# One chain of heads across the blocks of a hybrid encoder layer, S5 constants in parts

## The chip, the cores and the metric

The kernel runs on one core of a Trainium2 chip. The metric is the device time of one execution in microseconds (us), lower being better. Engines are named as in the profile: PE is the matmul engine (TensorE), DVE is VectorE, ACT is ScalarE, POOL is GpSimd, and SP is SyncE, which issues nearly all DMAs here. "L120" is line 120 of the kernel before, unless the text says that it speaks of the changed one; behind line 292 a line of the changed kernel has a higher number (L813 has become L820, L852 has become L859, L1126 has become L1133).

## The reference

One layer of a streaming encoder, for 2048 tokens of a prompt and 32 tokens of a second group. All groups of heads read the same normalised input, and their outputs share one output projection:

```python
hn = rmsnorm(h, W['norm_mix'][i])
proj = hn @ W['w_in'][i]
qkv_pre, z, ba, u5, cc = jnp.split(proj, [OFF_Z, OFF_BA, OFF_S5, OFF_CC], axis=-1)
ya, s_gdn, b_gconv = gdn_mixer(qkv_pre, z, ba, ...)      # gated delta rule, 4 heads x 128, short conv
yb, s_s5 = s5_mixer(u5, ...)                             # diagonal state space scan, then a GLU
yc, b_conv = conformer_conv(cc, ...)                     # GLU, depthwise conv of width 31, LayerNorm, silu
mix = jnp.concatenate([ya, yb, yc], axis=-1)
h = h + mix @ W['w_out'][i]
hf = rmsnorm(h, W['norm_ffn'][i])
h = h + (jax.nn.silu(hf @ W['ffn_w1'][i]) * (hf @ W['ffn_w3'][i])) @ W['ffn_w2'][i]
h = h + (p[i] @ W['pe_w'][i]) * jax.nn.sigmoid(h @ W['pe_gate_w'][i])
```

The model has width 1024 and a hidden width of 2816. The gated delta rule and the S5 scan carry a state over the tokens; the convolution of width 31 needs the 30 rows ahead. Everything is in float32. Outputs are the normalised result and the new states of both groups.

## The kernel before

Tokens come in four blocks (b = 0 to 3) of 512; the last one has 32 more, the second group, and its products go in two pieces of 272 columns. Features lie on the partitions. A dense product (`dense`, L104) is made of three float32r products per block of 128 features: high part of the weight by high part of the input, low by high, and high by low. A product of eight features' blocks is thus 24 matmuls into one PSUM buffer; there are three such buffers, so PE can be three products ahead of their eviction. `load_weight` (L81) brings a weight: a load on SP, the high part by ACT (L94), the low part by POOL (L96) the first time, with a store that keeps it in DRAM (L100), and by a load of that (L93) in all later blocks.

The dense work has two phases. Phase A (`PhaseA.block`, L622) makes for each block the normalised input, then the products for S5 (u5), the gates of the delta rule (`gates`, whose last part ends in ps_gc, L780), the conformer's gated input xc, twelve weights of q, k and v with a short convolution behind each (`conv`, L592: raw, three taps on gacc, a tanh and a product), and four weights of z (zz, L730 and L733). Phase F (`PhaseF.block`, L1107; F0 to F3 below) loads the mixed heads of a block as hb (L1124), splits them into fah and fal, multiplies by w_out, and then makes the hidden layer (w1 and w3 by L1165 to L1173, w2 by L1187) and the gated embedding. F0 splits its weights on POOL; F1 to F3 load the low parts that F0 kept.

The heads themselves are generators, and they run between the dense products:
- `conformer_block` (conf_b): 62 taps of the depthwise convolution on DVE (two halves of 31, L813 and the operation ahead of it, accumulating in cacc), transposes on PE (ps_ct, L824), statistics, transposes back (ps_cf, L843), and two halves of the output (L846 to L852), cxn, which SP stores to mixT, the buffer in DRAM from which phase F loads hb. There is one buffer cxn, so that the second half waits for the first one's store.
- `gdn_group` (twice for each block; gdn_b): the chunked delta rule, whose first matmul with the solved chunk is ps_q (L982), behind a triangular solve on DVE that ends in XT (L961).
- `s5_init`: the constants of S5, made once (powers of lambda, PTre and PTim, the small convolution kernel kg and ps_kg, L352).
- `s5_unit` (S5_0 for blocks 0 and 1, S5_1 for blocks 2 and 3): four quarters, each with matmuls ps_v (L459), a scan and products on DVE and POOL that end in X and XD (L498, L500), and matmuls ps_y (L517, L518); after two quarters gq (L537), which the products of the GLU read (ps_glu, L547).

Two things set the order. First, `dense` calls `step`, which counts columns of matmuls, and after each STAGE = 9216 columns (18 matmuls of 512) moves every started chain on by one stage; `yield k` takes k stages. `flush` runs the chains to their end. Second, instructions have priorities by class ("first" ahead of "heads" ahead of "later"; weights are first, dense matmuls and the chains are later), and a scheduler makes from them, from the dependences and from the memory of the pools one fixed order for every engine. Each engine then runs its instructions in this order and waits at each for what it needs. A pool on the right side (R, for each head) takes memory that an earlier pool has freed.

In the kernel before, s5_init runs in one go between block 0 and block 1 of phase A, in the class "heads". One chain of conf_0 and gdn_0 is started behind it, S5_0 is started as a second chain ahead of block 2, and the chains are flushed behind block 3. Ahead of each F block b a chain of conf and gdn of block b + 1 is started, with S5_1 at the end of that of F0, and it is flushed behind the block.

Of the kernel before, what the change touches and what calls it, by code (L numbers as in the profile page):

```python
# [206 lines left out]
def s5_init(G, A, tp, pspool):  # L207
# [78 lines left out]
    for m in (1, 2, 4):  # L286
# [4 lines left out]
        cmul(nc, tmp, Lre[:, m + 1:2 * m + 1], Lim[:, m + 1:2 * m + 1], Lre[:, 1:m + 1], Lim[:, 1:m + 1], bre, bim)  # L291


    nre = t8("nre")
# [23 lines left out]
    cmul(nc, [x[:, :, :16] for x in big], Bre, Bim, bre0, bim0, bc(kre), bc(kim))  # L318


    C.Hre = cp.tile([P, 8, 9, 16], F32, tag="Hre", name="Hre")
# [3 lines left out]
    for l in range(9):  # L325
        tmp = [x[:, :, l * 16:(l + 1) * 16] for x in big]
        cmul(nc, tmp, C.Hre[:, :, l], C.nHim[:, :, l], cre0, cim0, bc(Lre[:, l]), bc(Lim[:, l]))
    V.tensor_scalar(C.nHim, C.nHim, -1.0, None, op0=ALU.mult)
    for l in range(8):
        tmp = [x[:, :, l * 16:(l + 1) * 16] for x in big]  # L330
        cmul(nc, tmp, Pre[:, :, l], Pim[:, :, l], Bre, Bim, bc(Lre[:, l]), bc(Lim[:, l]), eng=nc.gpsimd)

    C.PT = []
    for nm, src in (("PTre", Pre), ("PTim", Pim)):
# [25 lines left out]
    for l in range(8):  # L360
        nc.sync.dma_start(C.Toep[l * 16:(l + 1) * 16, :, (7 - l) * 16:P].rearrange("p g (l c) -> p g l c", c=16), kg[:, :, 0:l + 1])


    NC = G.UB * BLK // L5
# [11 lines left out]
    while m < NC:  # L376
        s3 = [P, 8, m]
        tmp = [x.rearrange("p a b -> p (a b)")[:, :8 * m].rearrange("p (a b) -> p a b", a=8) for x in big]
        cmul(nc, tmp, fre[:, :, m:2 * m], fim[:, :, m:2 * m], fre[:, :, 0:m], fim[:, :, 0:m],
             fre[:, :, m - 1:m].to_broadcast(s3), fim[:, :, m - 1:m].to_broadcast(s3))  # L380
        m *= 2
    a = big[0][:, :, :NC]
    b = big[1][:, :, :NC]
# [31 lines left out]
def s5_unit(G, A, u, wp, pspool):  # L415
# [14 lines left out]
    for jq in range(4):  # L430
# [17 lines left out]

        yield 2

# [54 lines left out]

        yield 2

        ys = wp.tile([P, 4, NCT], F32, tag="ys", name="ys")
        ysv = ys.rearrange("p (j h) c -> p j h c", h=2)
        for j0 in (0,):  # L510
            for h in range(2):
                p_ = pspool.tile([P, 512], F32, tag="pc", name="ps_y")
                for j in range(j0, j0 + 2):
                    g = 2 * j + h
# [22 lines left out]
        V.scalar_tensor_tensor(gq[:, jh], t, 1.0, yf, op0=ALU.add, op1=ALU.mult)  # L537
        yield 2
    spc = 512 // NCT
# [23 lines left out]
class PhaseA:  # L563
# [58 lines left out]
    def block(self, b):  # L622
# [76 lines left out]
        for j in range(2):  # L699
# [13 lines left out]
            if not last:  # L713
                nc.sync.dma_start(G.xcd[b + 1][:, j, 0:30], xc[:, BLK - 30:BLK])
        with G.later():
            for g in gs:
                for _ in g:
                    pass
        for h in range(NH):
            self.conv(4 + h, 2 * h, b, hf, hl_, bc, n, last, t0)  # L720
            self.conv(h, 2 * h + 1, b, hf, hl_, bc, n, last, t0)
        for h in range(NH):
            self.conv(8 + h, 8 + h, b, hf, hl_, bc, n, last, t0)
        for h in range(NH):
            w = load_weight(G, A.w_in[12 + h], KD, "z", h)
# [129 lines left out]
def gdn_group(G, A, sp, pspool, T, tw, nt, nw, S, b, c_out):  # L855
# [105 lines left out]
    V.transpose(XT.rearrange("p w c -> p (w c)"), X.rearrange("p w c -> p (w c)"))  # L961
    yield 3

# [263 lines left out]
def trunk_kernel(ctx: ExitStack, tc: tile.TileContext, A):  # L1227
    nc = tc.nc
    G = Ctx()
# [36 lines left out]

    def flush():
        while G.chains:
            G.chains = [c for c in G.chains if advance(c)]
# [101 lines left out]
    with ExitStack() as cx:  # L1371
        pa = PhaseA(G, A, cx)
        pa.block(0)
        with R("s5i") as tp, G.heads():
            s5_init(G, A, tp, G.psM)

        with R("s5_0") as w5:
            G.start(run(conf_of(0), gdn_of(0)))
            for b in range(1, NB):
                if b == G.UB:  # L1380
                    G.start(s5_unit(G, A, 0, w5, G.psM))
                pa.block(b)
            if NB == G.UB:
                G.start(s5_unit(G, A, 0, w5, G.psM))
            G.flush()
    pf = PhaseF(G, A, ctx)
    for b in range(NB):
        nb = b + 1
        if nb < NB:

            G.start(run(conf_of(nb), gdn_of(nb), *(s5_of(u) for u in range(1, G.NU) if max(u * G.UB - 2, 0) == b)))
        pf.block(b)
        G.flush()

# [114 lines left out]
```

## Time and profile before

| what | us |
|---|---|
| timed runs, lowest / median / highest | 2912.3 / 2914.17 / 2915.87 |
| the profiled execution: its own time | 2906.6 |
| the profiled execution: its span | 2904.8 |
| PE busy, share of the span | 2775.6, 96% |
| DVE busy | 1769.2, 61% |
| ACT busy / POOL busy | 931.4 / 625.4 |
| mean granted clock of PE | 0.976 of full speed |

The span runs from the first to the last instruction; the profiled execution's own time is 1.8 longer, and the median of the timed runs is 7.6 above that. A row of the timeline gives the start, the length, the engine, the line and the operation as out<-in, the count, and in brackets how long the engine had stood idle and what released it. A row of the groups gives the busy time and the mean in ns behind the first bar. A row of the windows gives start:end, the length, and the busy time of PE, of its weight loads, of DVE, ACT and POOL, with counts, then the granted clock, the share of the DMA engines and GB/s. Phase A ends at some 706 us, with the last product of z; F0 ends at about 1300.

### The profile page before, as it was taken

How to read it: one execution, taken by the hardware profiler on the slowest of the kernel's cores; microseconds unless marked ns; L12 is line 12 of the kernel's file. 1: busy time of each engine (PE TensorE's matmuls, PEld its weight loads, DVE VectorE, ACT ScalarE, POOL GpSimd, SP SyncE). 2: the span in 40 equal slices, each digit the busy share in tenths (PEclk: the TensorE clock that was granted, in tenths of full speed). 3: DMA queues.
4: the chain of work that ended last, by engine and by line, in shares of the span. 5: the costliest groups of instructions: out<-in, count | busy, mean ns of one | idle time of the engine just before them, and what ended most of it. 6: DMA issues, size and time to landing. Idle time of an engine off the chain costs nothing.

```text
span 2904.8 us, 40874 instructions
## 1 busy us (share of the span) xinstructions
PE 2775.6 (96%) x15300; PEld 2373.5 (82%) x15300; DVE 1769.2 (61%) x3812; ACT 931.4 (32%) x1382; POOL 625.4 (22%) x482
## 2 busy tenths in 40 slices
PE   7789999899999999898999999999999999999997
PEld 5668777798878778676888887888888789999997
DVE  8989768896675856676663645954454543333343
ACT  4244433334322222233322323432222343222232
POOL 5733222133543434441010100110000010000000
PEclk9989999999999999899999999999999999999998
DMA  6577776657654546565565656765565574555553
GB/s 217 186 261 245 234 206 222 190 169 242 218 176 161 187 152 225 172 205 204 190 199 160 208 167 222 243 203 179 186 190 167 178 269 158 175 174 175 175 188 104
DMA packets 280566, 565.16 MB, mean 195 GB/s; under 512 B 68993, under 2 KB 128529, under 8 KB 280225
## 3 DMA queue, kind: packets, MB, share of 16 engines
q1 hardware_dynamic: 280368, 562.55, 60.1%
q8 instruction: 121, 1.98, 0.3%
q14 instruction: 77, 0.62, 0.1%
HBM read 457.67 MB, written 104.20 MB: 193 GB/s over the span
## 4 chain that ended last, share of the span: by engine, by line
PE 73%; DVE 14%; DMA 8%; issue 2%; SPq 2%; ACT 1%; POOL 0%; DVEq 0%; ACTq 0%; POOLq 0%
PE ps_d L120 65%; DVE gacc L614 1%; DVE cx L952 1%; DMA sild<-gacc 1%; DMA cu<-ud 1%; DVE ct L951 1%; PE ps_q L982 1%; DMA xk<-in_xT 1%; DMA mixT<-zy 1%; PE ps_z L995 1%; DVE cacc L813 1%; PE ps_kk L904 1%; DMA zy<-zgd 1%; DVE X L498 1%; PE ps_ks L1025 1%
## 5 line engine op out<-in xcount | busy, mean ns | idle before, releaser
L94 ACT ACTIVATE wh_w<-wr_w 128x1024 fp32r<-128x1024 f32 (+1 forms) x272 | 281.3, 1034 | 841.3 <-PE ps_d L120 596.5
L120 PE MATMUL ps_d<-fah,wh_w 128*128 128x512 f32 (+1 forms) x1760 | 382.0, 355 | 7.8 <-DVE hb L1142 3.4
L120 PE MATMUL ps_d<-fal,wh_w 128*128 128x512 f32 (+1 forms) x1760 | 379.2, 354 | 0.0
L120 PE MATMUL ps_d<-fah,wl_w 128*128 128x512 f32 (+1 forms) x1760 | 375.5, 352 | 0.0
L120 PEld LDWEIGHTS ps_d<-fah,wh_w 128*128 128x128 f32 x1760 | 290.7, 189 | 52.4 <-issue 4.9
L120 PEld LDWEIGHTS ps_d<-fal,wh_w 128*128 128x128 f32 x1760 | 291.4, 189 | 42.7
L120 PEld LDWEIGHTS ps_d<-fah,wl_w 128*128 128x128 f32 x1760 | 290.8, 188 | 42.8
L1187 DVE TENSOR_TENSOR hb<-hb,ps_d 128x512 f32<-128x512 f32 (+1 forms) x240 | 140.1, 585 | 181.7 <-PE ps_d L120 180.7
L120 PE MATMUL ps_d<-acth,wh_w 128*128 128x512 f32 (+1 forms) x880 | 208.3, 355 | 8.0 <-DVE hb L1187 4.5
L96 POOL TENSOR_TENSOR wl_w<-wr_w,wh_w 128x1024 fp32r<-128x1024 f32 (+1 forms) x68 | 160.7, 2365 | 237.3 <-ACT wh_w L94 229.5
L120 PE MATMUL ps_d<-acth,wl_w 128*128 128x512 f32 (+1 forms) x880 | 209.4, 354 | 0.0
L120 PE MATMUL ps_d<-actl,wh_w 128*128 128x512 f32 (+1 forms) x880 | 209.1, 355 | 0.0
L813 DVE SCALAR_TENSOR_TENSOR cacc<-xc,cc_w,cacc 128x512 f32<-128x512 f32 (+1 forms) x240 | 178.8, 779 | 0.0
L120 PEld LDWEIGHTS ps_d<-acth,wh_w 128*128 128x128 f32 x880 | 148.8, 189 | 34.3 <-DVE hb L1187 6.9
L120 PEld LDWEIGHTS ps_d<-actl,wh_w 128*128 128x128 f32 x880 | 150.1, 190 | 22.4
L120 PEld LDWEIGHTS ps_d<-acth,wl_w 128*128 128x128 f32 x880 | 149.8, 189 | 22.3
L1170 DVE SCALAR_TENSOR_TENSOR fth<-ps_d,bc 128x512 f32<-128x512 f32 (+1 forms) x110 | 64.8, 589 | 135.4 <-PE ps_d L120 134.8
L1165 DVE TENSOR_TENSOR fa<-ps_d,bc 128x512 f32<-128x512 f32 (+1 forms) x110 | 64.7, 589 | 128.8 <-PE ps_d L120 115.5
L1168 DVE SCALAR_TENSOR_TENSOR fa<-fth,fa 128x512 f32<-128x512 f32 (+1 forms) x110 | 92.3, 839 | 73.4 <-ACT fth L1167 73.2
L614 DVE SCALAR_TENSOR_TENSOR gacc<-raw,cw,gacc 128x512 f32<-128x512 f32 (+1 forms) x144 | 118.9, 828 | 27.4 <-ACT gacc L612 24.8
L1173 DVE TENSOR_TENSOR actl<-fa,acth 128x512 fp32r<-128x512 f32 (+1 forms) x110 | 85.5, 778 | 48.6 <-ACT acth L1172 48.4
L120 PE MATMUL ps_d<-hh,wl_qkv 128*128 128x512 f32 (+1 forms) x480 | 108.2, 362 | 5.9 <-POOL wl_qkv L96 5.9
(468 smaller groups left out, 4817.1 us busy)
## 6 DMA issues: line engine op xcount, KB each, us to landing
wr_w<-in_w SPq DMA_DIRECT2D x256, 512.0 KB, 4.0
wl_w<-lo_w SPq DMA_DIRECT2D x192, 512.0 KB, 3.5
lo_w<-wl_w SPq DMA_DIRECT2D x64, 512.0 KB, 3.0
wr_qkv<-in_w_in SPq DMA_DIRECT2D x48, 512.0 KB, 4.0
wl_qkv<-lo_qkv SPq DMA_DIRECT2D x36, 512.0 KB, 4.3
wr_out<-in_w_out SPq DMA_DIRECT2D x32, 512.0 KB, 4.9
wr_gate<-in_pe_gate SPq DMA_DIRECT2D x32, 512.0 KB, 4.6
sild<-gacc SPq DMA_DIRECT2D x48, 256.0 KB, 4.1
```

The costliest lines, as they stand in the source:

```text
L94: nc.scalar.activation(wh, wr, AF.Copy)
L96: nc.gpsimd.tensor_tensor(wl, wr, wh.bitcast(F32), op=ALU.subtract)
L120: nc.tensor.matmul(ps[:, :cn], a[:, i, :], x(k)[:, c0:c0 + cn], start=start and p_ == 0 and i == 0, stop=stop and p_ == 2 and i == K - 1)
L498: V.tensor_tensor(X[h][half[i], :, 1:], a[half[h], :, :NC], b_[half[h], :, :NC], op=op)
L614: V.scalar_tensor_tensor(acc, raw[:, t:t + W], cw[:, m, t:t + 1], acc, op0=ALU.mult, op1=ALU.add)
L813: V.scalar_tensor_tensor(acc[:, j], xc[:, j, t:t + W], cn_.w[:, j, t:t + 1], acc[:, j], op0=ALU.mult, op1=ALU.add)
L904: nc.tensor.matmul(kk4[:, h - h0], kq[:, 2 * h, cw], kq[:, 2 * h:2 * h + 2, cw], start=True, stop=True)
L1165: V.tensor_tensor(a, p1[:, :cn], bc[:, cs], op=ALU.mult)
L1168: V.scalar_tensor_tensor(a, th, 1.0, a, op0=ALU.add, op1=ALU.mult)
L1170: V.scalar_tensor_tensor(th, p3[:, :cn], 0.5, bc[:, cs], op0=ALU.mult, op1=ALU.mult)
L1173: V.tensor_tensor(fb[:, cs], a, fa[:, cs].bitcast(F32), op=ALU.subtract)
L1187: V.tensor_tensor(hb[m][:, c0:c0 + cn], hb[m][:, c0:c0 + cn], p_[:, :cn], op=ALU.add)
```

## The change

There are four edits.
1. The S5 constants become stages: `s5_init` gets eight places with a yield, and it is the first part of one chain, `first_heads`, which is started behind block 0 and goes on with gdn_0 and then conf_0 (conf_0 was first). S5_0 is a chain of its own, `first_s5`, that waits until the constants are done.
2. In phase F one chain, `later_heads`, goes through conf_b, S5_1 (at b = 2, between conf_2 and gdn_2) and gdn_b for b = 1 to 3. Ahead of block b the chains run on only until block b's heads are done (`ready`), and what is left of the chain goes on over the border.
3. More stages between parts: 3 for 2 ahead of ps_v, 4 for 2 ahead of ps_y, 1 or 5 for 2 behind gq, and 5 for 3 ahead of ps_q.
4. The rest of the gates in `PhaseA.block` is written behind the q, k and v convolutions.

```diff
@@ s5_init (and five more yields: behind the powers of lambda, in the loops, ahead of the scan constants)
+    yield 2
     C.PT = []
@@ s5_unit
-        yield 2
+        yield 3
         w = [wp.tile([P, 2, NCT], F32, tag=f"w{i}", name=f"w{i}") for i in range(2)]
...
-        yield 2
+        yield 4
         ys = wp.tile([P, 4, NCT], F32, tag="ys", name="ys")
...
-        yield 2
+        yield 1 if jh == 0 else 5
@@ PhaseA.block
-        with G.later():
-            for g in gs:
-                for _ in g:
-                    pass
         for h in range(NH):
             self.conv(4 + h, 2 * h, b, hf, hl_, bc, n, last, t0)
             self.conv(h, 2 * h + 1, b, hf, hl_, bc, n, last, t0)
         for h in range(NH):
             self.conv(8 + h, 8 + h, b, hf, hl_, bc, n, last, t0)
+        with G.later():
+            for g in gs:
+                for _ in g:
+                    pass
@@ gdn_group, behind the solve
-    yield 3
+    yield 5
@@ trunk_kernel
-    def flush():
-        while G.chains:
+    def flush(done=lambda: False):
+        while G.chains and not done():
             G.chains = [c for c in G.chains if advance(c)]
@@
-        with R("s5i") as tp, G.heads():
-            s5_init(G, A, tp, G.psM)
-        with R("s5_0") as w5:
-            G.start(run(conf_of(0), gdn_of(0)))
-            for b in range(1, NB):
-                if b == G.UB:
-                    G.start(s5_unit(G, A, 0, w5, G.psM))
-                pa.block(b)
...
+        def first_s5():
+            while "w5" not in box:
+                yield 1
+            yield from s5_unit(G, A, 0, box["w5"], G.psM)
+            box["done"] = True
+        def first_heads():
+            with R("s5i") as tp:
+                yield from s5_init(G, A, tp, G.psM)
+            with R("s5_0") as w5:
+                box["w5"] = w5
+                yield from gdn_of(0)
+                yield from conf_of(0)
+                while "done" not in box:
+                    yield 1
+        G.start(first_heads())
+        for b in range(1, NB):
+            if b == G.UB:
+                G.start(first_s5())
+            pa.block(b)
...
+    def later_heads():
+        for b in range(1, NB):
+            yield from conf_of(b)
+            if b % G.UB == 0:
+                yield from s5_of(b // G.UB)
+            yield from gdn_of(b)
+            ready[0] = b
+    G.start(later_heads())
     for b in range(NB):
-        nb = b + 1
-        if nb < NB:
-            G.start(run(conf_of(nb), gdn_of(nb), *(s5_of(u) for u in range(1, G.NU) if max(u * G.UB - 2, 0) == b)))
+        G.flush(lambda: ready[0] >= b)
         pf.block(b)
-        G.flush()
```

What this does to the fixed order shows at three places. The first is DVE at the end of phase A. In the kernel before the last gacc, the statistics of conf_1 (cst, cmv, cve) and the evictions of z follow one another, and fal of F0 comes next:

```order
L614 SCALAR_TENSOR_TENSOR gacc<-raw,cw,gacc 128x547 x5
L617 SCALAR_TENSOR_TENSOR gacc<-gth,gacc 128x547
L614 SCALAR_TENSOR_TENSOR gacc<-raw,cw,gacc 128x547
L617 SCALAR_TENSOR_TENSOR gacc<-gth,gacc 128x547
L827 BN_STATS cst<-ctk 128x6
L828 BN_AGGR cmv<-cst 128x2
L827 BN_STATS cst<-ctk 128x6
L828 BN_AGGR cmv<-cst 128x2
L730 TENSOR_TENSOR zz<-ps_d,bc 128x272 x2
```

In the changed kernel, on the same engine, with the last four evictions of z (zz, now L737) and the first statistics of conf_0:

```order
L737 TENSOR_TENSOR zz<-ps_d,bc 128x272
L820 SCALAR_TENSOR_TENSOR cacc<-xc,cc_w,cacc 128x512 x5
L740 SCALAR_TENSOR_TENSOR zz<-zth,zz 128x544
L737 TENSOR_TENSOR zz<-ps_d,bc 128x272
L820 SCALAR_TENSOR_TENSOR cacc<-xc,cc_w,cacc 128x512 x2
L737 TENSOR_TENSOR zz<-ps_d,bc 128x272
L820 SCALAR_TENSOR_TENSOR cacc<-xc,cc_w,cacc 128x512 x5
L740 SCALAR_TENSOR_TENSOR zz<-zth,zz 128x544
L820 SCALAR_TENSOR_TENSOR cacc<-xc,cc_w,cacc 128x512 x43
L834 BN_STATS cst<-ctk 128x6
```

Taps of both conf_0 and conf_1 now stand between the last convolutions and z, and 43 of them behind the last zz; the last 34 of these are conf_0's. In the kernel before conf_0's 62 taps stand at the border of blocks 0 and 1.

The second place is SP at the same point. In the kernel before the loads of hb from block 0's mixT (mixT_59) stand among the weights and the stores of phase A:

```order
L1124 DMA hb<-mixT_59 128x512 x2
L88 DMA wr_z<-in_w_in 128x1024
L1124 DMA hb<-mixT_59 128x512 x6
L93 DMA wl_z<-lo_z_1194 128x1024
L618 DMA sild_66<-gacc 128x512
L620 DMA sild_66<-gacc 128x32
```

In the changed kernel:

```order
L741 DMA zgd_70<-zz 128x544
L1104 DMA g_7065<-in_norm_ffn 128x8
L1106 DMA g_7067<-in_norm_final 128x8
L859 DMA mixT_59<-cxn 128x512 x2
L1131 DMA hb<-mixT_59 128x512 x7
L1133 DMA hb<-in_xT 128x512
L1131 DMA hb<-mixT_59 128x512
```

The two stores of conf_0's output are the last thing ahead of the loads of hb, and both are behind all stores of z. On PE, between the last product of z and the first with fah, there stand only the eight ps_ct and eight ps_cf of conf_0 and then those of conf_1.

The third place is PE at the border of F0 and F1, where the last quarter of S5_1 is in the kernel before (ps_y, then the products of F1's w_out with fah and fal, and ps_ss, the sum of squares that closes F0):

```order
L517 MATMUL ps_y<-ug,c_Toep 128x4
L518 MATMUL ps_y<-XD_11335,c_G 128x4
L120 MATMUL ps_d<-fal,wh_gate 128x512 x5
L120 MATMUL ps_d<-fah,wh_out 128x512 x8
L120 MATMUL ps_d<-fah,wl_out 128x512 x6
L547 MATMUL ps_glu<-gq,glu 128x396 x2
```

In the changed kernel the first quarter of S5_1 begins behind that border:

```order
L149 MATMUL ps_ss<-ones,ssum_11221 128x1 x4
L120 MATMUL ps_d<-fal,wh_out 128x512 x7
L120 MATMUL ps_d<-fah,wh_out 128x512 x8
L120 MATMUL ps_d<-fah,wl_out 128x512 x8
L120 MATMUL ps_d<-fal,wh_out 128x512 x7
L132 MATMUL ps_bc<-ident,rso 128x128 x4
L120 MATMUL ps_d<-fal,wh_out 128x512
L120 MATMUL ps_d<-fah,wh_out 128x512 x3
L466 MATMUL ps_v<-ug,c_PT 64x132 x8
```

All four quarters of S5_1 have moved from F0 into F1, and conf_2 has taken their place in F0.

More of the change, by code (lines that the diff above doesn't have):

```diff
@@ L327, in s5_init @@
         cmul(nc, tmp, C.Hre[:, :, l], C.nHim[:, :, l], cre0, cim0, bc(Lre[:, l]), bc(Lim[:, l]))
+        if l % 3 == 2:
+            yield 1
     V.tensor_scalar(C.nHim, C.nHim, -1.0, None, op0=ALU.mult)
@@ L361, in s5_init @@
         nc.sync.dma_start(C.Toep[l * 16:(l + 1) * 16, :, (7 - l) * 16:P].rearrange("p g (l c) -> p g l c", c=16), kg[:, :, 0:l + 1])
+    yield 1
     NC = G.UB * BLK // L5
@@ L381, in s5_init @@
         m *= 2
+        yield 1
     a = big[0][:, :, :NC]
@@ L1373, in trunk_kernel @@
         pa.block(0)
-        with R("s5i") as tp, G.heads():
-            s5_init(G, A, tp, G.psM)
-        with R("s5_0") as w5:
-            G.start(run(conf_of(0), gdn_of(0)))
-            for b in range(1, NB):
-                if b == G.UB:
-                    G.start(s5_unit(G, A, 0, w5, G.psM))
-                pa.block(b)
-            if NB == G.UB:
-                G.start(s5_unit(G, A, 0, w5, G.psM))
-            G.flush()
-    pf = PhaseF(G, A, ctx)
+        box = {}
+        def first_s5():
+            while "w5" not in box:
+                yield 1
+            yield from s5_unit(G, A, 0, box["w5"], G.psM)
[8 more added lines that the diff above has]
+                while "done" not in box:
+                    yield 1
+        G.start(first_heads())
[3 more added lines that the diff above has]
+            pa.block(b)
+        if NB == G.UB:
+            G.start(first_s5())
+        G.flush()
+    pf = PhaseF(G, A, ctx)
+    ready = [0]
+    def later_heads():
[6 more added lines that the diff above has]
+    G.start(later_heads())
     for b in range(NB):
-        nb = b + 1
-        if nb < NB:
-            G.start(run(conf_of(nb), gdn_of(nb), *(s5_of(u) for u in range(1, G.NU) if max(u * G.UB - 2, 0) == b)))
+        G.flush(lambda: ready[0] >= b)
         pf.block(b)
-        G.flush()
 def _layout(np, d):
```

## Prediction

> **What bounds the kernel now.** I read the engines' busy times first, then the busy time by stage, then what the matmul engine waits for, and then the timeline at the places that the change touches.
>
> ```profile
> PE 2775.6 (96%) x15300; PEld 2373.5 (82%) x15300; DVE 1769.2 (61%) x3812; ACT 931.4 (32%) x1382; POOL 625.4 (22%) x482
> ```
>
> PE is busy for 96% of the span, and the change leaves its matmuls as they are. So there are only 129 us of idle time (2904.8 less 2775.6) and the time lost at a lowered clock to win, and any amount to lose. Where this lies, the windows show (start:end, length, busy time of each engine, then the granted clock):
>
> ```profile
> 0.00:72.60 72.60, 56.52 (x221) 41.59 (x222) 63.67 (x200) 31.00 (x47) 40.82 (x26) 0.95 0.67 217
> 72.60:145.20 72.60, 57.85 (x262) 45.64 (x260) 71.07 (x158) 19.23 (x30) 55.88 (x72) 0.91 0.56 186
> 145.20:217.90 72.70, 61.87 (x243) 45.68 (x244) 59.58 (x87) 29.14 (x44) 27.38 (x19) 0.86 0.79 261
> 217.90:700.00 482.10, 457.77 (x2716) 393.73 (x2715) 386.51 (x954) 179.14 (x288) 126.54 (x156) 0.98 0.68 212
> 1161.90:1234.50 72.60, 60.50 (x270) 49.76 (x270) 45.05 (x91) 18.49 (x28) 32.31 (x20) 0.84 0.57 172
> 1234.50:1307.20 72.70, 69.03 (x326) 56.54 (x323) 53.22 (x103) 25.96 (x39) 30.00 (x19) 0.93 0.62 205
> 1307.20:1379.80 72.60, 60.72 (x251) 47.39 (x251) 48.96 (x69) 27.26 (x38) 10.06 (x6) 0.93 0.60 204
> 1379.80:2904.80 1525.00, 1501.03 (x8836) 1322.40 (x8834) 738.31 (x1657) 465.56 (x681) 101.42 (x76) 0.99 0.58 186
> ```
>
> Three stages can give something back: block 0 of phase A and its border with block 1 (14.8 and 10.8 us idle at clocks of 0.91 and 0.86, with VectorE busy for 71.07 of 72.6 us), blocks 1 to 3 (24.3 us idle), and the end of F0 (12.1, 3.7 and 11.9 us idle). The last row, over half the span, has only 24 us. The waits behind these (waiting operation, the releaser, us in total, times, longest):
>
> ```profile
> PE ps_y L518 <- DVE X L498: 13.7, 3, 5.5
> PE ps_glu L547 <- DVE gq L537: 8.7, 2, 6.4
> PE ps_d L120 <- POOL wl_qkv L96: 5.9, 1, 5.9
> PE ps_bc L132 <- DVE rso L70: 5.6, 2, 3.4
> PE ps_gc L780 <- issue: 5.1, 1, 5.1
> PE ps_q L982 <- DVE XT L961: 4.7, 2, 3.5
> PE ps_kg L352 <- ACT kg L354: 4.4, 1, 4.4
> PE ps_q L982 <- DVE g_p L771: 4.2, 1, 4.2
> ```
>
> **Phase A, block 0: a gain of 16.** The rest of the gates goes behind the convolutions and the S5 constants come in parts as stages of the chain, so ps_gc and ps_kg meet operands that are long done: 5.1 + 4.4 go. At the border of blocks 0 and 1 there are also waits for zz, because conf0's taps share VectorE with it. The waits of the first 218 us alone:
>
> ```profile
> PE ps_d L120 <- DVE zz L730: 6.9, 2, 4.2
> ```
>
> The taps leave this place, and I take 6.5 of the 6.9. The wait of 5.9 for POOL's wl_qkv stays, since that step stands behind the same POOL rows as before. Sum 5.1 + 4.4 + 6.5 = 16. At the low end only ps_gc and part of ps_kg go (8), at the high end all idle time of the two windows but the 5.9 and the clock with it (30).
>
> **Phase A, blocks 1 to 3: a gain of 15.** Idle are 24.3, of which 4.9 belong to the border. VectorE is lighter by conf0's 62 taps in block 1, and gdn_group has five stages instead of three ahead of ps_q: the waits for g_p (4.2), the longer one for XT (3.5) and for rso (3.4) go, with about 4 of smaller ones: 15. Bounds 5 and 25: only XT and part of another, or all idle time and some clock.
>
> **F0 and F1: a gain of 27.** S5_1 ran in F0, where POOL splits weights (L96); now it comes behind conf2 and runs over the border into F1, where the low parts are loaded. What POOL does to VectorE stands in these rows (start, length, operation, wait):
>
> ```profile
> 1148.19 1.12 PE L459 MATMUL ps_v<-ug,c_PT 128*64 128x132 f32 x16
> 1161.48 2.57 DVE L498 TENSOR_TENSOR X<-tm,tm 64x256 f32<-64x256 f32 x1
> 1167.31 0.80 PE L518 MATMUL ps_y<-X,c_G 128*128 128x128 f32 x2 [5.53 <-DVE X L498]
> ```
> ```profile
> 1274.16 1.12 PE L459 MATMUL ps_v<-ug,c_PT 128*64 128x132 f32 x16
> 1284.55 0.79 DVE L498 TENSOR_TENSOR X<-tm,tm 64x256 f32<-64x256 f32 x1
> 1286.52 0.42 DVE L498 TENSOR_TENSOR X<-tm,tm 64x256 f32<-64x256 f32 x1
> 1287.49 0.38 PE L518 MATMUL ps_y<-X,c_G 128*128 128x128 f32 x2
> ```
>
> The first quarter took 19.1 us from ps_v to ps_y with its wait of 5.5; the fourth, where few POOL operations fell in, 13.3 and no wait. The extra yields do little: the order counts 51, 48, 54 and 51 matmuls of ps_d between the last ps_v and the first ps_y<-X in before, and 75, 47, 55 and 49 now. So it is POOL's absence that takes the 13.7 away, not the spacing. The ps_glu that waited longest stood 112 matmuls of ps_d behind the last ps_y and stands 92 behind it now; of its 8.7 I leave 3. That is 13.7 + 5.7 = 19.4. The clock comes on top: 0.84, 0.93 and 0.93 of three windows are at most 11.6 + 5.1 + 5.1 us, some of it idle anyhow; I take 7.6. Sum 27, bounds 15 (POOL's tail still touches the first two quarters) and 36 (idle time all gone).
>
> **The border from phase A to F: a loss of 66.** This is the other side. In before conf0's 62 taps are done at the first border of phase A, and only conf1's lie in block 3. Now the first chain runs S5 constants, gdn0, conf0 in this order, and conf1's taps still come in block 3, so both sets stand in its last weights, 43 taps in a row behind the last zz; on SP the eight loads of hb for F0 stand behind conf0's two stores, and PE has nothing between z and ps_d<-fah but ps_ct and ps_cf. Prices (count, then busy time and mean ns):
>
> ```profile
> L813 DVE SCALAR_TENSOR_TENSOR cacc<-xc,cc_w,cacc 128x512 f32<-128x512 f32 x180 | 130.4, 757 | 0.0
> L617 DVE SCALAR_TENSOR_TENSOR gacc<-gth,gacc 128x547 f32<-128x547 f32 x12 | 8.6, 719 | 1.6 <-ACT gth L616 1.6
> L730 DVE TENSOR_TENSOR zz<-ps_d,bc 128x272 f32<-128x272 f32 x8 | 3.4, 437 | 7.5 <-PE ps_d L120 6.7 <-DMA sild<-gacc 0.8
> ```
> ```profile
> 1363.90 5.38 DVE L813 SCALAR_TENSOR_TENSOR cacc<-xc,cc_w,cacc 128x512 f32<-128x512 f32 x8
> ```
>
> Eight taps in a row took 5.38, and each next one starts 0.664 after the last. Behind the eviction of the last convolution VectorE has 87 taps (44 among the zz, then the 43): 57.8; eleven operations on 544 or 547 columns, gacc's last taps and the products with tanh, at 0.72: 7.9; eight zz of 0.44: 3.5. Sum 69.2, of which PE covers the four z weights. Rows of these, with the wait that before has there:
>
> ```profile
> 688.68 2.18 PE L120 MATMUL ps_d<-hh,wh_z 128*128 128x272 f32 x8 [4.93 <-DVE zz L730]
> 694.28 1.37 PE L120 MATMUL ps_d<-hh,wh_z 128*128 128x272 f32 x8
> 703.53 1.17 PE L120 MATMUL ps_d<-hh,wh_z 128*128 128x272 f32 x8
> 706.56 1.03 PE L843 MATMUL ps_cf<-ident,ctk 128*128 128x128 f32 x8
> ```
>
> 24 matmuls take 3.03 (703.53 to 706.56), so eight groups take 24.2. Behind the taps comes conf0's tail, which before shows at 258:
>
> ```profile
> 258.15 0.60 PE L824 MATMUL ps_ct<-ident,cacc 128*128 128x128 f32 x4
> 277.74 0.78 ACT L846 ACTIVATE cxn<-ps_cf,cc_bb,cc_g 128x512 f32<-128x512 f32 x1 [0.73 <-DMA mixT<-cxn]
> 279.22 0.69 DVE L851 SCALAR_TENSOR_TENSOR cxn<-cth,cxn 128x512 f32<-128x512 f32 x1 [0.64 <-ACT cth L850]
> 279.94 0.32 SPq L852 DMA_DIRECT2D mixT<-cxn  x1
> hb<-mixT SPq DMA_DIRECT2D x24, 256.0 KB, 6.7
> ```
>
> From ps_ct to the second store it took 21.8 (258.15 to 279.94) among other work; with VectorE, ScalarE and POOL free I estimate 14 to 18 from the steps in it; the load of hb adds 4 to 6.7, and fah about 1. I take 23, with 19 and 29 as its ends. So PE stands still for 69.2 + 23 - 24.2 = 68.0; 3.2 of that are ps_ct and ps_cf of both blocks, which before pays too, and before's own loss here goes: 4.9 of wait and 2.6 of clock (its 24 matmuls from 688.68 took 5.60 instead of 3.03). That leaves 57.3. Added are the lag of VectorE when the last convolution ends (0 to 10, since the taps already stand among the convolutions; I take 3), one ramp of the clock, 2.6, and POOL's three splits of wl_out among the taps. These are priced by this pair:
>
> ```profile
> 701.87 2.41 POOL L96 TENSOR_TENSOR wl_out<-wr_out,wh_out 128x1024 fp32r<-128x1024 f32 x1 [3.79 <-ACT wh_out L94]
> 702.37 2.49 DVE L733 SCALAR_TENSOR_TENSOR zz<-zth,zz 128x544 f32<-128x544 f32 x1 [1.20 <-ACT zth L732]
> ```
>
> An operation of some 0.72 took 2.49 beside a split: three cost 0 to 5.3, I take 3. Sum 65.9, so 66; bounds 54 and 80.
>
> The Trainium skill's page SBUF — State Buffer, in "SBUF: two separate sides", calls the pair of ports that VectorE and GpSimd share an exclusive lock, held for the whole instruction by whoever comes first, where the VectorE operation has two SBUF inputs. The pair of rows above agrees; by the rule every split would meet a tap, and the sum would be 68 instead of 66. The page TensorE: Matmul & The Clock Gate, in "What's actually happening", gives about 3.4 us of half speed after an idle window, an estimated 1.7 lost; the trace has 2.6 and decides.
>
> **The sum.** -16 - 15 - 27 + 66 = +8. On the profiled execution's 2906.6 this is 2914.6. The three timed runs lie higher, their median 7.6 above that execution, so 2914.17 + 8 = 2922.
>
> **The rivals.**
> - The waits weigh more than the border (faster). If VectorE's relief ends all of phase A's idle time that is not POOL's or the border's, at 30 + 25, and F gives 33, 88 stand against 66: -22, 2892. For it speaks VectorE's 71.07 of 72.6; against it, that its steps there remain and only move into block 1. It decides from the point at which the gains pass 66, or the border falls under 58 at gains of 58. Chance 0.30.
> - The gains stay away (slower by more). VectorE's load in block 0 is S5 constants and gates as much as taps, and the spacing in F hardly grows. With the lower bounds 8 + 5 + 15 = 28 against 66 it is +38, 2952. For it speak the counted matmuls; against it, the idle POOL in F1. Chance 0.20.
> - The order of the heads changes nothing (the change doesn't do what it says): if the 43 taps had found covered time, as conf1's do in before, the border would cost nothing and the time be 2914 - 58 = 2856. The order of PE leaves no dense product there, so I give it 0.02 and leave it outside the range.
>
> **How the numbers follow.** The forecast's case has 0.48; it is centred on +8 and reaches from about -6 to +22. A measurement of this kernel tells 0.2%, 5.8 us, from no change. Of the 0.48, 0.18 lie within that and 0.30 above; with the rivals that is faster 0.32, same 0.18, slower 0.50. The range goes from 2888 (the first rival's time and a little) to 2952 (the second's).
>
> **What would show it.** In the changed kernel's trace I expect one idle stretch of PE of 55 to 75 us at the end of phase A, ended by fah of F0, with VectorE on cacc and then idle; ps_kg and the early ps_gc without waits; ps_y without waits near the start of F1 and X at 0.4; and the 5.9 for wl_qkv still there. The forecast is wrong if that stretch is under 40, or if the first 218 us keep their 36 to 42 us of idle time.

## The result, and the profile after

The changed kernel is slower: a median of 2951.11 us (2946.76 to 2953.24, four runs) against 2913.78 of before (2912.3 to 2915.87, four runs), a ratio of 1.0126 with a 95% interval of 1.0108 to 1.0143. That is 37 us where 8 were forecast. It lies within the range, but only just: its upper end is 2952. The profiled execution of the changed kernel has a span of 2951.1, 46.3 above that of before, so that some 9 us of the 46.3 are spread between executions. Profiles are compared with profiles, and times by their medians or ratios. In a second, slower state an execution takes longer at a lower granted clock (the profiled one of conf2_behind_s5 took 3075.09 us at 0.839 and isn't read); all ratios below are of the fast runs alone.

The engines' busy times of the changed kernel:

```profile
PE 2766.7 (94%) x15300; PEld 2362.6 (80%) x15300; DVE 1777.0 (60%) x3812; ACT 933.1 (32%) x1382; POOL 609.2 (21%) x482
```

PE has as many instructions as before and 8.9 us less busy time (the granted clock is higher in three of the four windows below); it stands idle for 184.4 us instead of 129.2. The difference of these, 55.2 - 8.9, is the 46.3. Where it arose, the windows show. First the kernel before, in windows that hold most of block 0, blocks 1 to 3, the border from phase A to F, and F0 with F1:

```profile
72.60:217.90 145.30, 119.72 (x505) 91.32 (x504) 130.65 (x244) 48.37 (x73) 83.26 (x91) 0.88 0.68 224
217.90:650.00 432.10, 412.70 (x2381) 349.08 (x2380) 355.33 (x893) 162.53 (x262) 117.12 (x134) 0.98 0.68 211
650.00:800.00 150.00, 145.07 (x819) 128.21 (x819) 97.44 (x143) 59.73 (x87) 62.45 (x47) 0.98 0.67 228
800.00:1453.00 653.00, 613.73 (x2874) 500.64 (x2873) 432.54 (x764) 186.63 (x265) 224.87 (x116) 0.96 0.57 186
```

The same windows of the changed kernel:

```profile
72.60:217.90 145.30, 124.23 (x552) 96.60 (x551) 118.17 (x227) 51.63 (x77) 78.87 (x92) 0.92 0.66 218
217.90:650.00 432.10, 416.65 (x2484) 357.81 (x2482) 313.29 (x819) 161.98 (x258) 87.73 (x134) 0.99 0.70 220
650.00:800.00 150.00, 75.93 (x386) 64.18 (x387) 114.03 (x178) 33.90 (x54) 50.26 (x31) 0.72 0.40 134
800.00:1453.00 653.00, 622.20 (x2960) 507.61 (x2960) 452.43 (x773) 198.11 (x280) 249.77 (x123) 0.98 0.57 189
```

PE's idle time (length less busy time) fell by 4.5 in block 0, by 4.0 in blocks 1 to 3 and by 8.5 in F0 and F1. It rose from 4.9 to 74.1 at the border. These windows have the same times in both kernels, but not the same work: behind the border the changed kernel is some 60 us late. So here is also the length of each stage, from the start of its first dense product on PE to that of the next stage's (matmuls of the heads move from stage to stage with the chains):

| stage | before | changed | difference |
|---|---|---|---|
| block 0, up to u5 of block 1 | 195.7 | 190.8 | -4.9 |
| blocks 1 and 2, up to u5 of block 3 | 334.8 | 308.8 | -26.0 |
| block 3, up to z | 143.6 | 159.4 | +15.8 |
| z of block 3, up to F0's first product with fah | 33.2 | 107.6 | +74.3 |
| F0 | 584.4 | 564.4 | -20.1 |
| F1 | 544.1 | 547.4 | +3.3 |
| F2 and F3, up to the end | 1068.9 | 1072.8 | +3.9 |

All other stages together gained 28.0, and the border lost 74.3. PE's waits by cause, of the changed kernel:

```profile
PE ps_ct L831 <- DVE cacc L820: 37.7, 2, 37.4
PE ps_d L120 <- DVE raw L614: 23.3, 5, 6.3
PE ps_d L120 <- DVE zz L737: 20.9, 2, 19.2
PE ps_d L120 <- DVE hb L1194: 13.5, 8, 3.0
PE ps_cf L850 <- POOL ctk L847: 9.1, 2, 4.6
PE ps_q L989 <- DVE XT L968: 7.2, 2, 4.8
PE ps_d L120 <- DVE fth L1177: 4.3, 1, 4.3
PE ps_d L120 <- POOL wl_qkv L96: 2.0, 1, 2.0
PE ps_y L525 <- DVE X L505: 0.7, 1, 0.7
```

The waits that the prediction named are nearly all gone: X from 13.7 to 0.7, and ps_glu, ps_gc, ps_kg and g_p from 22.4 together to nothing. But raw, which had 2.4, has 23.3, and hb of w2 has 13.5 instead of 5.5. The border, first on PE, then on DVE, POOL and SP:

```profile
687.34 2.18 PE L120 MATMUL ps_d<-hh,wh_z 128*128 128x272 f32 x8 [19.16 <-DVE zz L737]
745.67 1.35 PE L831 MATMUL ps_ct<-ident,cacc 128*128 128x128 f32 x4 [37.44 <-DVE cacc L820]
753.03 2.30 PE L850 MATMUL ps_cf<-ident,ctk 128*128 128x128 f32 x8 [4.63 <-POOL ctk L847]
766.53 7.13 PE L120 MATMUL ps_d<-fah,wh_out 128*128 128x512 f32 x22
```
```profile
677.37 1.40 DVE L820 SCALAR_TENSOR_TENSOR cacc<-xc,cc_w,cacc 128x512 f32<-128x512 f32 x2
686.84 0.79 DVE L737 TENSOR_TENSOR zz<-ps_d,bc 128x272 f32<-128x272 f32 x2 [8.08 <-DMA sild<-gacc]
694.12 2.87 DVE L820 SCALAR_TENSOR_TENSOR cacc<-xc,cc_w,cacc 128x512 f32<-128x512 f32 x1
704.24 5.20 DVE L820 SCALAR_TENSOR_TENSOR cacc<-xc,cc_w,cacc 128x512 f32<-128x512 f32 x5
710.36 3.14 DVE L820 SCALAR_TENSOR_TENSOR cacc<-xc,cc_w,cacc 128x512 f32<-128x512 f32 x2
717.71 28.56 DVE L820 SCALAR_TENSOR_TENSOR cacc<-xc,cc_w,cacc 128x512 f32<-128x512 f32 x43
```
```profile
664.73 14.09 POOL L615 COPY tails<-raw 128x3 f32<-128x3 f32 x1 [4.19 <-DVE raw L614]
```
```profile
663.55 0.42 SPq L627 DMA_DIRECT2D sild<-gacc  x1
678.84 0.34 SPq L743 DMA_DIRECT2D out_gconv_p<-tails  x1
680.70 0.38 SPq L625 DMA_DIRECT2D sild<-gacc  x1
757.34 4.86 SPq L859 DMA_DIRECT2D mixT<-cxn  x2
762.25 3.28 SPq L1131 DMA_DIRECT2D hb<-mixT  x7
```

The 43 taps in a row took 28.56, and PE stood for 37.4 until they were done. Conf_0's tail went from the last tap (746.3) to the first product with fah (766.53), 20.3 us. The wait of 19.2 ahead of that ends with the eviction zz at 686.84, which came late because VectorE had taps ahead of it, and because of a wait of 8.1 that I had not seen, at the end of a short chain. POOL's copy of three columns into tails, which takes 0.19 in the median, began at 664.73 and took 14.09: it ended at 678.82, when VectorE, which until then had gone from tap to tap, paused (677.37 + 1.40 = 678.77). SP's store of tails waited for that copy, from 663.97 to 678.84; sild's store stands behind it on SP (680.70), though its gacc was done at 674.09; and that store frees the buffer of gacc which VectorE needs for zz at 686.84. The chain so held the store back for up to 6.6, and I estimate that without it the wait of 8.1 would have been some 1.5. In no_taps_conf0 (below) the copy took 4.77, up to VectorE's next operation with a single input in SBUF, and the wait for sild was 2.1:

```profile
659.82 4.77 POOL L615 COPY tails<-raw 128x3 f32<-128x3 f32 x1 [4.20 <-DVE raw L614]
```
```profile
664.46 0.41 DVE L834 BATCH_NORM_STATS2 cst<-ctk 128x6 f32<-128x256 f32 x1
```

In conf1_behind_gdn1, where operations of the gates stand among the taps, the last such copy took 0.71.

### The profile page after: what moved, and what is told of

Its sections match the earlier page's. It is cut to its first block, busy times and chain, and to the rows that moved or that the text cites. A ratio compares the mean times of both kernels' runs of the same rounds, so it can differ in the third digit from the quotient of the medians.

```text
span 2951.1 us, 40881 instructions
## 1 busy us (share of the span) xinstructions
PE 2766.7 (94%) x15300; PEld 2362.6 (80%) x15300; DVE 1777.0 (60%) x3812; ACT 933.1 (32%) x1382; POOL 609.2 (21%) x482
## 4 chain that ended last, share of the span: by engine, by line
PE 70%; DVE 17%; DMA 7%; issue 3%; SPq 1%; ACT 1%; POOL 0%; DVEq 0%; ACTq 0%; POOLq 0%
PE ps_d L120 62%; DVE cacc L820 4%; DVE gacc L621 1%; DMA xk<-in_xT 1%; DVE ct L958 1%; DVE cx L959 1%; PE ps_q L989 1%; PE ps_kk L911 1%; DMA mixT<-zy 1%; PE ps_z L1002 1%; DMA sild<-gacc 1%; DVE hb L1194 1%; DMA cu<-ud 1%; PE ps_vn L1045 1%; PE ps_s L1052 1%
## 5 line engine op out<-in xcount | busy, mean ns | idle before, releaser
L820 DVE SCALAR_TENSOR_TENSOR cacc<-xc,cc_w,cacc 128x512 f32<-128x512 f32 (+1 forms) x240 | 198.7, 870 | 0.0
L120 PE MATMUL ps_d<-hh,wh_qkv 128*128 128x512 f32 (+1 forms) x480 | 110.2, 370 | 20.7 <-DVE raw L614 20.5
```

Source lines behind the costliest of these rows:

```text
L120: nc.tensor.matmul(ps[:, :cn], a[:, i, :], x(k)[:, c0:c0 + cn], start=start and p_ == 0 and i == 0, stop=stop and p_ == 2 and i == K - 1)
L820: V.scalar_tensor_tensor(acc[:, j], xc[:, j, t:t + W], cn_.w[:, j, t:t + 1], acc[:, j], op0=ALU.mult, op1=ALU.add)
```

## The experiments

Each kernel's ratio is to runs of the kernel before that were timed beside it (medians of 2908.88 to 2909.66; 2913.78 for the changed kernel). The ratios, with their 95% intervals:

| kernel | median us | ratio | interval |
|---|---|---|---|
| the changed kernel | 2951.11 | 1.0126 | 1.0108 to 1.0143 |
| conf0_first | 2907.01 | 0.9995 | 0.9984 to 1.0006 |
| constants_early | 2905.18 | 0.9989 | 0.9976 to 1.0002 |
| no_taps_conf0 | 2901.46 | 0.9966 | 0.9953 to 0.9979 |
| conf1_behind_gdn1 | 2942.27 | 1.0106 | 1.0089 to 1.0123 |
| conf2_behind_s5 | 2912.46 | 1.0007 | 0.9995 to 1.0020 |
| later_chain_only | 2889.66 | 0.9934 | 0.9920 to 0.9948 |
| s5_kept_in_f0 | 2907.96 | 0.9996 | 0.9986 to 1.0006 |
| conf2_late_only | 2886.73 | 0.9924 | 0.9902 to 0.9945 |
| gates_behind | 2893.38 | 0.9938 | 0.9916 to 0.9960 |
| later_conf1_behind | 2913.93 | 1.0019 | 1.0006 to 1.0031 |
| yields_only | 2911.75 | 1.0012 | 1.0003 to 1.0021 |
| constants_in_parts | 2944.20 | 1.0122 | 1.0101 to 1.0143 |

The theory: the border costs 66 because conf_0's taps come behind gdn_0 and so beside conf_1's, and the rest of the change gains 58. Its rivals: the border waits for a late chain whatever its order, and the gains are not there. Idle times at the border below are those of PE from 650 to 800 us.

**conf0_first**: the order of the first chain alone.

```diff
-                yield from gdn_of(0)
                 yield from conf_of(0)
+                yield from gdn_of(0)
```

> The changed kernel with one edit: in the first chain conf_0 runs ahead of gdn_0 again. If the loss is conf_0's taps behind the last zz (the theory), the idle time of PE at the end of phase A falls from some 80 us to 15 or less and the time from 2951 to 2880-2890. If the hole is there because all heads of block 0 come later (S5 constants ahead of them), gdn_0 takes conf_0's place as the last thing ahead of hb, and the time stays over 2925.

The ratio fell from 1.0126 to 0.9995, by 38 us of 2910. The theory has most of it, but not all: the time is not 2880 to 2890, and the border kept waits. PE at the border of this kernel:

```profile
657.63 2.18 PE L120 MATMUL ps_d<-hh,wh_z 128*128 128x272 f32 x8 [5.80 <-DVE zz L737]
708.10 1.97 PE L1085 MATMUL ps_ot<-ident,o 128*128 128x128 f32 x8 [7.09 <-DVE o L1077]
722.72 6.73 PE L120 MATMUL ps_d<-fah,wh_out 128*128 128x512 f32 x21 [12.65 <-ACT fah L1110]
```

Now gdn_0 is last: its output (o, ps_ot), its two stores to mixT and the load of hb. PE is idle for 30.2 in the window of the border, against 4.9 in before and 74.1 with gdn_0 first. So the order of the two heads decides 44 of the 69 in the profile. The other 25 come from a chain that is late whatever its order: by constants_early and yields_only (below) the constants in parts make some 14 of them and the raised yields 11.

**no_taps_conf0**: 60 of conf_0's 62 taps are left out.

```diff
-        for t in range(1, TAPS):
+        for t in range(1, TAPS if b else 1):
```

> The changed kernel without the 60 taps of conf_0's convolution (each half keeps its first product with one weight; conf_1 to conf_3 are whole). It leaves work out, to measure what conf_0's taps cost at the border of phase F. Theory: the wait of ps_ct for cacc (37 us) and most of the wait for zz (19) are VectorE's time on taps, so some 40 to 55 us go and the time is 2896-2911. Rival: the border waits for the late end of the chain (gdn_0, then conf_0's statistics, output and the load of hb), and only 10 to 20 us go: 2931-2941.

The ratio fell by 0.0160, 47 us, in the middle of the theory's range. PE's idle time at the border fell from 74.1 to 25.5, by 48.6. Of these, 60 taps at 0.664 are 39.8, the shorter wait for sild (2.1 for 8.1) is 6, and one of POOL's splits no longer meets a tap. So nearly all of it is VectorE's time on the taps. The edit also takes out the ten yields between conf_0's taps, which brings its later parts forward in the order (its ps_ct stand among the products of z here); what that alone is worth isn't separated.

**conf1_behind_gdn1**: the other half of the taps.

```diff
         for b in range(1, NB):
-            yield from conf_of(b)
+            if b > 1:
+                yield from conf_of(b)
             if b % G.UB == 0:
                 yield from s5_of(b // G.UB)
             yield from gdn_of(b)
+            if b == 1:
+                yield from conf_of(b)
             ready[0] = b
```

> The changed kernel with conf_1 behind gdn_1 in the later chain, so that conf_1's taps leave block 3 and only conf_0's stand at the border; 27 instead of 43 taps are left behind the last zz. Theory (the sum of both convolutions on VectorE): 20 to 30 us of the border go, 2921-2931. Rival (conf_0's place behind gdn_0 alone decides): 2945 or more. F0 can lose up to 10 by taking conf_1's taps among POOL's splits.

Neither forecast was met: its ratio, 1.0106, cannot be told from that of the changed kernel. The windows say why: idle at the border fell from 74.1 to 47.0, by 27, as the theory has it, and rose by 7.3 in F0 and F1 and by 3.6 behind it. PE's busy time, summed over its windows, is 10.0 longer as well, and so the span is only 6.3 shorter. The sum on VectorE is right, then, but conf_1's taps have to be somewhere: by the stages of the two profiles the border is 33.1 shorter, F0 20.5 longer and F2 10.7 longer.

**later_conf1_behind**: the same edit on later_chain_only (below), where the border has no hole.

> later_chain_only with conf_1 behind gdn_1. Blocks 1 to 3 lose conf_1's 41 us of VectorE work: if that is what zz, raw and xc wait for there, 5 to 12 go, 2878-2885. If F0 gives it back (conf_1's taps then lie among POOL's splits, with waits for hb and fth): 2888-2896.

It is slower than later_chain_only by 0.0085, 25 us, and so outside both forecasts. By stages of the two profiles, F0 is 22.4 longer (580.2 for 557.9), F2 13.0 longer, and phase A 8.1 shorter. F2's part isn't explained. The waits early in F0 of this kernel, where conf_1's 62 taps now are:

```profile
759.24 3.75 PE L120 MATMUL ps_d<-fah,wh_w 128*128 128x512 f32 x8 [5.33 <-DVE hb L1142]
782.48 3.78 PE L120 MATMUL ps_d<-fah,wh_w 128*128 128x512 f32 x8 [6.08 <-DVE fa L1165]
```

**later_chain_only**: the kernel before with edit 2 of the change alone (`later_heads`, `ready` and the conditional flush, as in the diff above).

> The kernel before with one edit: phase F's one chain over the borders (conf_1, gdn_1, conf_2, S5_1, gdn_2, conf_3, gdn_3); constants, gates and yields as before. As predicted (S5_1 away from POOL's splits is worth 27): 2885-2890. If, as the profile after suggests, conf_2's taps now stand among POOL's splits and give half of it back: 2898-2905, with no waits for X but 8-15 us of waits for hb of w2 in F0.

19 us faster (0.9934). In us that falls in the first forecast; counted as a ratio from the 2914 that the prediction used, it is 2895 and lies between the two: 27 less what came back. PE's waits of its F0 and F1 (800 to 1453 us):

```profile
PE ps_d L120 <- DVE hb L1187: 13.3, 9, 3.0
PE ps_q L982 <- DVE XT L961: 4.7, 2, 3.4
PE ps_d L120 <- DVE fth L1170: 4.3, 1, 4.3
PE ps_y L518 <- DVE X L498: 0.7, 1, 0.7
```

X and gq, which have 20.1 in this window of before, are down to 0.7, and hb of w2 has risen from 4.5 to 13.3, with 4.3 for fth beside it.

**s5_kept_in_f0**: is it S5_1's place, or that the chain isn't flushed at the border?

```diff
         for b in range(1, NB):
-            yield from conf_of(b)
             if b % G.UB == 0:
                 yield from s5_of(b // G.UB)
+            yield from conf_of(b)
             yield from gdn_of(b)
```

> later_chain_only with S5_1 ahead of conf_2, so that S5_1 stays in F0 among POOL's splits and conf_2 in F1, while one chain still goes over the borders. If the 20 us that the later chain gains come from S5_1 leaving the splits (the theory), they are gone: 2903-2912, and the three waits for X are back. If they come from the chain that is no longer flushed at the border: 2886-2895.

All of the gain is gone (0.9996), and the waits are back, in number and size:

```profile
PE ps_y L518 <- DVE X L498: 14.0, 3, 4.8
PE ps_glu L547 <- DVE gq L537: 9.3, 2, 6.7
```

The longest operation that makes X takes 2.60 here, beside a split, and 0.80 in later_chain_only, where S5_1 lies in F1. So what the later chain gains is S5_1 out of F0. A chain over the border is worth nothing by itself.

**conf2_late_only**: later_chain_only with gdn_2, S5_1 and then conf_2.

```diff
         for b in range(1, NB):
-            yield from conf_of(b)
             if b % G.UB == 0:
+                yield from gdn_of(b)
                 yield from s5_of(b // G.UB)
-            yield from gdn_of(b)
+                yield from conf_of(b)
+            else:
+                yield from conf_of(b)
+                yield from gdn_of(b)
             ready[0] = b
```

> The later chain in another order (gdn_2, S5_1, conf_2 in place of conf_2, S5_1, gdn_2), nothing else; conf_2's taps then lie in F1, away from POOL's splits. If the taps beside the splits cost F0 10 to 13 us (waits for hb of w2 and for fth): 2876-2882. If gdn_2 among the splits costs as much, or the waits have another cause: 2888-2895.

The waits for hb of w2 halved (13.3 to 6.7) and fth's went, but the ratio, 0.9924, is within the interval of later_chain_only's 0.9934, and the time lies between the two forecasts. In the window of F0 and F1 other waits came: those of ps_q for XT rose from 4.7 to 8.7 (a third one, of 3.1, is gdn_2's, which now lies in F0), and there is one of 3.2 for fa. F0 is 10.2 longer than in later_chain_only and F1 7.8 shorter. **conf2_behind_s5** is the same edit on conf0_first:

> conf0_first with a second edit: in the later chain gdn_2 comes first, then S5_1, then conf_2, so that conf_2's 62 taps lie in F1, where POOL splits no weights. If the taps beside the splits cost 10 to 13 us, this is 10 to 13 below conf0_first, at 2870-2880, and the waits for hb of w2 in F0 go. If those waits have another cause (the order of the chain as such), it is level with conf0_first.

It, too, is level with conf0_first (1.0007 and 0.9995, with overlapping intervals).

**gates_behind**: later_chain_only with edit 4.

```diff
-        with G.later():
-            for g in gs:
-                for _ in g:
-                    pass
         for h in range(NH):
             self.conv(4 + h, 2 * h, b, hf, hl_, bc, n, last, t0)
...
+        with G.later():
+            for g in gs:
+                for _ in g:
+                    pass
         for h in range(NH):
             w = load_weight(G, A.w_in[12 + h], KD, "z", h)
```

> The later chain and the gates behind the convolutions, nothing else. If ps_gc's wait of 5 is worth what it was counted for: 4 to 6 below later_chain_only, 2884. If VectorE is what bounds block 0, the wait only changes its name to raw, and the time is level with later_chain_only, 2888-2892.

No gain (0.9938). PE's waits between 72 and 218 us, of this kernel:

```profile
PE ps_d L120 <- DVE zz L730: 12.1, 2, 10.7
PE ps_d L120 <- DVE raw L607: 9.2, 3, 7.9
PE ps_d L120 <- POOL wl_qkv L96: 6.1, 1, 6.1
```

ps_gc's 5.1 is gone, ps_kg's is down to 0.6, and raw and zz have taken 12 more than they had in later_chain_only (0.9 and 8.5). VectorE is busy for 130.62 of the 145.3 us here, as before.

**yields_only**: edit 3 on the kernel before.

```diff
-        yield 2
+        yield 3
         w = [wp.tile([P, 2, NCT], F32, tag=f"w{i}", name=f"w{i}") for i in range(2)]
-        yield 2
+        yield 4
         ys = wp.tile([P, 4, NCT], F32, tag="ys", name="ys")
-        yield 2
+        yield 1 if jh == 0 else 5
-    yield 3
+    yield 5
     hb = SB
```

> The kernel before with the four raised yields alone. If spacing does little, as the counts of the order say: 2908-2920. If the spacing is what takes the waits for X, XT and gq away: 2885-2900. In the order conf_1's taps also slip from ahead of z into z, which could cost up to 10 us at the border: then 2920-2930.

Some 3 us slower (1.0012). X's waits went from 13.7 to 8.9, though S5_1 is still in F0, and XT's from 4.7 to 6.6, while the border lost 11 (idle 15.9 against 4.9): the longer chain moves conf_1's taps into z, as the order said.

**constants_early**: the changed kernel with the S5 constants and the first chain as before (edits 2, 3 and 4).

> The changed kernel with the S5 constants as in the kernel before (in one go, class heads) and the first chain as before, conf_0 then gdn_0; the raised yields, the gates behind the convolutions and the later chain stay. Beside conf0_first (2907) it tells what the constants in parts do. If they delay the whole first chain and so leave the 45 us of excess at the border of phase F, the excess falls to some 20 and the time to 2895-2900, though the first 218 us lose again what they had gained (8). If the raised yields delay the chain, the border stays at 40 or more and the time is 2910-2920.

0.9989, level with conf0_first and between the two forecasts. The border has 16.3 of idle time, as in yields_only, against 30.2 in conf0_first; block 0 has 29.5 against 20.7. The constants in parts lighten block 0 by 9 and cost the border 14. (In the kernel's code their yields stand at six places, not eight.)

**constants_in_parts**: edits 1 and 2, with conf_0 ahead of gdn_0; yields and gates as before.

> The later chain and the S5 constants in parts, first chain constants, conf_0, gdn_0; yields and gates as before. If the constants in parts delay the chain, gdn_0 ends last and the border of phase F costs 25 or more above later_chain_only, partly paid by blocks 0 to 2 (up to 17): 2895-2905. If the delay comes from the raised yields, the border stays at 9 and the time is 2870-2880.

My expectation was far off: 1.0122, where 0.995 to 0.998 was the worse case. PE at its border:

```profile
712.70 3.67 PE L989 MATMUL ps_q<-XT,U 128*128 128x64 f32 x16 [15.44 <-DVE XT L968]
746.68 1.97 PE L1085 MATMUL ps_ot<-ident,o 128*128 128x128 f32 x8 [6.68 <-DVE o L1077]
760.92 7.66 PE L120 MATMUL ps_d<-fah,wh_out 128*128 128x512 f32 x22 [12.28 <-ACT fah L1110]
```

A whole group of gdn_0, from its solve on, lies behind the last product of z, with nothing on PE beside it. More was lost ahead of that: from u5 of block 1 to z of block 3 this kernel takes 476.7 and conf0_first 448.4, 28 more, and from there to F0's first product 91.2 against 81.8. PE's idle time from 217.9 to 650 us is 35.6, against 19.4 in before. Why the chain is later here than in conf0_first, which has more stages, I could not tell: the scheduler's order differs in many places, and no run separates them.

## Why the prediction was right or wrong

The direction and the mechanism of the border were right, and the sum of the gains was wrong: by stages they came to 28.0 where 58 were forecast, and the border to 74.3 where 66 were. The forecast's own case reached to +22; the result is +37. It stands where the second rival, "The gains stay away (slower by more)", had its price (gains of 28, 2952), with a chance of 0.20. That the time came within 1 us of that price is luck: the rival had the border at 66, and the two profiles differ by 46.3 where the medians differ by 37.

Of the signs that the prediction named, two speak against it. The first 218 us kept 38.0 us of idle time, within the 36 to 42 that it called wrong. The idle stretch is 58.3 long from the last z to fah, but PE has 9.5 us of ps_ct and ps_cf in it; the longest single wait is 37.4, under the 40, and ends with ps_ct. Ps_kg and the early ps_gc have no waits, as foreseen; X took 0.80 and then 0.42, where 0.4 was; the 5.9 for wl_qkv did not stay whole.

- **The border, 66 forecast, 74.3 measured.** Shown by conf0_first and no_taps_conf0. PE's idle time rose by 69.1 there. The taps (43 in 28.56) and the tail (20.3 against 23) were about right. Three terms were too small. The lag was taken as 3: the last convolution's product ended on PE at 659.14 and its eviction on VectorE at 664.70, 5.6 later. The wait of 8.1 for sild was in no term. POOL's three splits met three taps or runs of them: 2.87 for 0.74, 5.20 for 3.40 and 3.14 for 1.40 (at 0.664 a tap) make 5.7, where I took 3, with 5.3 as the end. The Trainium skill's SBUF — State Buffer ("SBUF: two separate sides") calls the ports that the two engines share an exclusive lock; that every split would meet a tap, as the prediction worked out from it, came true in this trace.
- **Phase A, block 0: 16 forecast, 4.5 of idle time measured** between 72.6 and 217.9 us, and a clock of 0.92 instead of 0.88; the stage is 4.9 shorter. The step that failed is "ps_gc and ps_kg meet operands that are long done: 5.1 + 4.4 go". They went, and zz went, but the wait changed its name: these are PE's waits of the changed kernel between 72 and 218 us:

```profile
PE ps_d L120 <- DVE raw L614: 18.9, 4, 6.3
PE ps_d L120 <- POOL wl_qkv L96: 2.0, 1, 2.0
```

  In before the same window had 22.3 in zz, wl_qkv, ps_gc and ps_kg. gates_behind shows the same by itself. VectorE was the limit of that stage, as its 71.07 of 72.6 had said: from 72.6 to 145.2 us it is busy for 71.87 in the changed kernel, and PE's idle time is 14.7 against 14.8. A wait of PE ahead of such an engine was not a gain to be counted one by one. The 4.5 come from the rest of the window, the border with block 1, where the waits for zz (6.9) went. Also, wl_qkv's 5.9 did not stay whole: PE came to it 3.8 later, from a wait for raw.
- **Blocks 1 to 3: 15 forecast, 10.2 measured up to z of block 3** (26.0 won in blocks 1 and 2, 15.8 lost in block 3, where the late chains run), and 4.0 of idle time in the window. "VectorE is lighter by conf0's 62 taps" was so (313.29 busy against 355.33). Of the waits that were to go, g_p's 4.2 went. Rso's 3.4 stayed, at 3.6. XT's 3.5 was misread: it stands at 1035.54 us, in F0. That the two more stages ahead of ps_q won anything is not shown: XT's waits grew in yields_only, and from 4.7 to 7.2 in the changed kernel.
- **F0 and F1: 27 forecast, 19 by later_chain_only**, and 16.8 by the stages of the changed kernel. That S5_1's place in F0 makes the 13.7 is shown by s5_kept_in_f0. "So it is POOL's absence that takes the 13.7 away, not the spacing" was half right: the operations on X that a split stretched to 2.5 or 2.6 are down to 0.80 in F1, but yields_only, with S5_1 still in F0, took 4.8 of the 13.7 away by spacing. I failed to price what takes S5_1's place. These are conf_2's taps in F0, in the changed kernel, and the POOL split that one of them met:

```profile
1213.93 3.17 POOL L96 TENSOR_TENSOR wl_w<-wr_w,wh_w 128x1024 fp32r<-128x1024 f32 x1 [5.62 <-ACT wh_w L94]
1214.76 2.89 DVE L820 SCALAR_TENSOR_TENSOR cacc<-xc,cc_w,cacc 128x512 f32<-128x512 f32 x1
1225.67 2.05 PE L120 MATMUL ps_d<-acth,wh_w 128*128 128x512 f32 x4 [4.33 <-DVE fth L1177]
1261.70 0.57 PE L120 MATMUL ps_d<-acth,wh_w 128*128 128x512 f32 x1 [2.87 <-DVE hb L1194]
```

  That 62 more taps in F0 make PE wait is shown (later_conf1_behind: F0 is 22.4 longer); how much of it is the splits, and how much the taps' own 41 us on VectorE, is not. Nor is it shown that moving them out of F0 would win the time back (conf2_late_only).
- **The edits do not add up.** Beside later_chain_only the constants in parts cost 55 (constants_in_parts), but together with the raised yields and the moved gates only 18 (conf0_first). Why isn't known; the edits shift where the first chain ends.

Of the runs, later_chain_only and conf2_late_only beat both kernels, by 19 and 22 us of the kernel before, with edit 2 alone; gates_behind, with edit 4 added, by 18.

## What to carry to other kernels

When work is moved from one stage to another, sum the busy time of the engine that carries it in the stage where it arrives, up to the next point where all must be done, and only then count the waits that go. Look also at what moves into the place that falls free. In a stage whose helper engine is busy for nearly all of the time, a wait of the matmul engine that is removed comes back under another name. What a chain of side work has to deliver at a border should be ordered by how long its last part takes to arrive there, with the stores and loads behind it.

## What the runs showed of the hardware

A POOL subtraction of 128x1024 held up a VectorE tap when the two met: one of 0.74 took 2.87 and another 2.89. The other way about was new to me: a run of two-input operations on VectorE without a gap kept POOL's copy of 128x3 waiting for 14.09 us, until VectorE paused, and for 4.77 in no_taps_conf0, until VectorE came to an operation with one input. The Trainium skill's SBUF — State Buffer ("SBUF: two separate sides") says that a VectorE operation with two inputs in SBUF and a GpSimd operation that reads SBUF exclude each other, and that whichever starts first keeps the shared pair of ports for the whole instruction. The trace agrees, and shows beyond it that the next VectorE operation can follow without POOL getting its turn, some twenty times in a row. A tiny copy on POOL is thus no cheap link in a chain that stores wait for, where VectorE is dense.
